# Where the output products of the last column groups stand, in a six-layer decoder kernel on one core

## The chip, the cores and the metric

The kernel runs on one NeuronCore of a Trainium2 chip. The time is device time of one execution in microseconds (us); less is better. The matmul engine is called PE (its weight loads PEld), the vector engine DVE, the activation engine ACT, GpSimd POOL; SP issues the DMA transfers.

## The reference

256 tokens of width 1024, all float32. A first block of two layers, each with a hybrid mixer, a cross attention on a memory and a squared-ReLU MLP, every part followed by a layer norm; then a second block of four layers, each with a mixer (retention, dilated attention, gMLP, retention), a SwiGLU FFN and a gated embedding, with RMS norms. Cut to the parts that the change touches:

```python
def squared_relu_mlp(x, w1, w2):            # two layers; w1 1024x4096, w2 4096x1024
    h = jnp.square(jax.nn.relu(jnp.einsum('bsd,df->bsf', x, w1)))
    return jnp.einsum('bsf,fd->bsd', h, w2)

def _swiglu(h, w_in, w_out):                # four layers; hidden width 2816
    gate, up = jnp.split(h @ w_in, 2, axis=-1)
    return (jax.nn.silu(gate) * up) @ w_out

def _retention_mixer(h, w_in, w_out):       # layers 0 and 3; four heads of value width 512
    ...
    return (jax.nn.silu(g) * y) @ w_out

def _gmlp_mixer(h, w_in, ln_g, ln_b, w_s, b_s, w_out):   # layer 2; width 2048
    ...
    return (u * s) @ w_out
```

## The kernel before, in words

The 256 tokens are two tiles of 128. Each tile is a Python generator, `thread(0)` and `thread(1)`, called t0 and t1 here. All weights come from HBM in 840 **blocks** of at most 512 KB, in the order of one list, `plan`: a `colblock` is a quarter of the rows of 512 columns, a `rowblock` is 128 rows of all 1024 columns. A block is loaded into one of five raw buffers (`load`, SP), then split into a high and a low float32r part (`split`: ACT writes `wh`, DVE writes `wl`), one block ahead of t0; 14 pairs of buffers hold the split halves, two to a block.

The loop at the end of the kernel sets the order: for each block, t0 takes a step with it, then t1 takes a step with a block some places earlier (`LAGS`: 4 in `ff1`, 3 in `ff2`, 1 in `rv`, `rg` and `gu`, 2 in `ro` and `go`, 5 in `fg` and `fu`, 4 in `fo`). A step is six products of 128x512 by `mm3` (high by high, high by low, low by high, for two halves).

An MLP, FFN, retention or gMLP goes by **column groups**. For group j the kernel computes the inputs (`in`: `proj` into a PSUM bank `pj`; four blocks in the MLP and the gMLP, eight in the FFN and the retention), makes the hidden values, and turns them by DMA, since the next product needs them transposed. This **trip** (`turn_by_dma`, `trip`) is: a DVE transpose of 32x32 pieces, four writes of 64 KB to DRAM (`xd<-xt`), one read back (`ffr<-xd`, `ffu<-xd`, `ro<-xd`, `gor<-xd`), and the split into the parts of the transposed operand (`part`, by ACT and DVE). The read back is put off until one step of the same thread later and the split until three steps later (`BACK, CUT = 1, 3`, counted by `flush`). Then the **output products** (`out`: `outproj`, accumulated in two PSUM banks `acc`; four blocks, two in the last group of the FFN, which is 256 wide) take the parts.

Before, the order within each of these stages is in 0, in 1, out 0, in 2, out 1, and so on, with the last two output groups behind the last input:

```python
for j in range(9):
    if j < 8:
        p = yield from proj(t, xT, ("ff1", l, j), 512)
        ...
        turn_by_dma(t, r_, 4, fT, j, IALPHA ** 0.5)
    if j > 0:
        yield from outproj(t, acc, ("ff2", l, j - 1), 4, fT, 4 * j - 4, j == 1, j == 8, ...)
```

After the last output product of a thread comes a norm (`layer_norm`, or `postnorm` and `prenorm`), whose result is transposed on PE (`xTp`) and split into the next stage's `part`. The transposed parts have eight buffers a thread: four pairs, of which the stage's own input `xT` holds two as long as inputs are left. The order of instructions on each engine follows this text with small shifts that the tile framework's scheduler makes; DVE, ACT, PE and the SP queue each work strictly in their order.

Of the kernel before, what the change touches and what calls it, by code (L numbers as in the profile page):

```python
# [15 lines left out]
P = 128  # L16
# [32 lines left out]
def kernel(  # L49
# [18 lines left out]
    tiles = {}  # L68
    shared = {}


    plan = []

# [7 lines left out]
    def rowblock(key, mat, kts):  # L81
        v = mat.rearrange("(k p) n -> p k n", p=P)
        for i, k in enumerate(kts):
            plan.append((key + (i,), "w", [P, 1, D], v[:, k:k + 1, :], None))
# [19 lines left out]
    for l in range(2):  # L104
        for nm, c0, n in MIXG:
            if nm == "cq" and l == 0:
                for t in range(2):
                    aux(("memr", t), "kv", [P, D], mem[t * P:(t + 1) * P, :])
            if nm == "cq":
                aux(("BT", l), "big8", [P, 6, 256], relx[l])  # L110
            colblock((nm, l), w_in[l], c0, n)
        for j in memory_blocks(l, "M"):
            colblock(("mkv", l, j), w_mkv[l], 512 * j, 512)
        rowblock(("mix", l), w_mix[l], MIXK)
        for which in range(3):
            if which == 0:
                fill(l, 0)
            if which == 1:
                for j in range(2):
                    colblock(("mq", l, j), w_mq[l], 512 * j, 512)  # L120
            if l == 1 and which == 2:
                aux(("lnGB",), "big8", [P, 2, D], bcast_row(ln_rows[l, which:which + 1, :, :]))
            if which == 1:
                rowblock(("mo", l), w_mo[l], list(range(8)))
                fill(l, 1)
            if which == 2:
                for j in range(9):
                    if j < 8:
                        colblock(("ff1", l, j), w_ff1[l], 512 * j, 512)
                    if j > 0:  # L130
                        rowblock(("ff2", l, j - 1), w_ff2[l], list(range(4 * j - 4, 4 * j)))
                fill(l, 2)
    FG = [(512 * j, min(512, 2816 - 512 * j)) for j in range(6)]
    for i in range(4):
        if i % 3 == 0:
            r = i // 3
            aux(("cb", i), "big8", [P, CB_W], cb)
            for nm, c0 in (("rq", 0), ("rk", 1024)):
                for j in range(2):
                    colblock((nm, i, j), ret_in[r], c0 + 512 * j, 512, (i, 0))  # L140
            for h in range(5):
                if h < 4:
                    colblock(("rv", i, h), ret_in[r], 2048 + 512 * h, 512, (i, 0))
                    colblock(("rg", i, h), ret_in[r], 4096 + 512 * h, 512, (i, 0))
                if h > 0:
                    rowblock(("ro", i, h - 1), ret_out[r], list(range(4 * h - 4, 4 * h)))
        elif i == 1:
            for hf in range(2):
                for g in range(3):
                    aux(("db", hf, g), "big8", [P, 8, 256], dilx[g, hf])  # L150
                    for c, nm in enumerate(("dq", "dk", "dv")):
                        colblock((nm, hf, g), att_in[0], 3072 * g + 1024 * c + 512 * hf, 512, (1, 0))
            for hf in range(2):
                rowblock(("do", hf), att_out[0], list(range(4 * hf, 4 * hf + 4)))
        else:
            aux(("gmg",), "big8", [P, 2048], bcast_row(gm_ln[0:1, :]))
            aux(("gmb",), "big8", [P, 2048], bcast_row(gm_ln[1:2, :]))
            aux(("gws",), "kv", [P, 8, P], gm_ws.rearrange("g n m -> n g m"))
            for j in range(4):
                colblock(("gv", j), gm_in[0], 2048 + 512 * j, 512, (2, 0))  # L160
            for j in range(5):
                if j < 4:
                    colblock(("gu", j), gm_in[0], 512 * j, 512, (2, 0))
                if j > 0:
                    rowblock(("go", j - 1), gm_out[0], list(range(4 * j - 4, 4 * j)))
        aux(("ng", i, 0), "grow", [P, D], bcast_row(ng_rows[i, 0:1, :]))
        for j in range(7):
            if j < 6:
                c0, n = FG[j]
                colblock(("fg", i, j), ffn_in[i], c0, n, (i, 1))  # L170
                colblock(("fu", i, j), ffn_in[i], 2816 + c0, n, (i, 1))
            if j > 0:
                c0, n = FG[j - 1]
                rowblock(("fo", i, j - 1), ffn_out[i], list(range(c0 // P, (c0 + n) // P)))
        aux(("ng", i, 1), "grow", [P, D], bcast_row(ng_rows[i, 1:2, :]))
        rowblock(("pp", i), ple_p[i], [0, 1])
        for j in range(2):
            colblock(("pg", i, j), ple_g[i], 512 * j, 512, (i, 2))
# [696 lines left out]
    def mlp(t, l, xT):  # L875
        acc = newacc(t)
        fT = Parts()
        for j in range(9):
            if j < 8:
                p = yield from proj(t, xT, ("ff1", l, j), 512)  # L880
                r_ = sb.tile([P, 512], F32, tag=f"rA{t}", name="ffr", bufs=2)
                V.tensor_scalar(out=r_, in0=p, scalar1=0.0, scalar2=None, op0=ALU.max)
                fT.banks.append(None)
                turn_by_dma(t, r_, 4, fT, j, IALPHA ** 0.5)
            if j > 0:
                yield from outproj(t, acc, ("ff2", l, j - 1), 4, fT, 4 * j - 4, j == 1, j == 8, xT if j == 1 else None)
        return acc


# [5 lines left out]
    def retention(t, i, hT, rs):  # L895
# [33 lines left out]
                turn_to(t, xf, 4, qT[j] if nm == "rq" else get2(("rkT", i, j), [P, 2, 4, P], "kv", 4)[:, t])  # L929
        acc = newacc(t)  # L930
        oT = Parts()
        for h in range(5):
            if h < 4:
                p = yield from proj(t, hT, ("rv", i, h), 512)
                vv = get2(("rv", i, h, t), [P, 512], f"U{t}", 3)
                S.activation(vv, p, AF.Copy, scale=rs[:, 0:1])
# [28 lines left out]
                V.scalar_tensor_tensor(out=o, in0=y, scalar=rr[:, 0:1], in1=th, op0=ALU.mult, op1=ALU.mult)  # L965
                oT.banks.append(None)
                turn_by_dma(t, o, 4, oT, h)
            if h > 0:
                yield from outproj(t, acc, ("ro", i, h - 1), 4, oT, 4 * h - 4, h == 1, h == 4)
        return acc  # L970

    def dilated(t, hT, rs):
# [95 lines left out]
    def gmlp(t, hT, rs):  # L1068
# [31 lines left out]
            (V if j == 0 else G).tensor_tensor(out=vs[j], in0=vs[j], in1=gb[:, sl], op=ALU.add)  # L1100
        acc = newacc(t)
        oT = Parts()
        for j in range(5):
            if j < 4:
                p = yield from proj(t, hT, ("gu", j), 512)
                u = sb.tile([P, 512], F32, tag=f"rA{t}", name="gur", bufs=2)
                S.activation(u, p, AF.Gelu, scale=rs[:, 0:1])
                sp = bank("tr", t, [P, 2, 256], "gsp")
                o = sb.tile([P, 512], F32, tag=f"rB{t}", name="gor", bufs=2)
                for k in range(2):  # L1110
                    g = 2 * j + k
                    T.matmul(sp[:, k, :], wsT[:, g, :], vs[j][:, 256 * k:256 * k + 256], start=True, stop=True)  # L1112
                for k in range(2):
                    g = 2 * j + k
                    V.scalar_tensor_tensor(out=o[:, 256 * k:256 * k + 256], in0=sp[:, k, :], scalar=gbs[:, g:g + 1],
                                           in1=u[:, 256 * k:256 * k + 256], op0=ALU.add, op1=ALU.mult)
                oT.banks.append(None)
                turn_by_dma(t, o, 4, oT, j)
            if j > 0:
                yield from outproj(t, acc, ("go", j - 1), 4, oT, 4 * j - 4, j == 1, j == 4)  # L1120
        return acc

    def swiglu(t, i, hT, rs):
# [4 lines left out]
        fT = Parts()  # L1128
        pT = shared[("pT", i, t)] = Parts()
        pT.banks.append(None)  # L1130
        for j in range(7):
            if j == 3:

                pr = sb.tile([P, 256], F32, tag=f"sc{t}", name="pr")
                nc.sync.dma_start(pr, p2[i, t * P:(t + 1) * P, :])
            if j == 4:
                turn_by_dma(t, pr, 2, pT, 0, at=21)
            if j < 6:
                n = FG[j][1]
                nkk = n // P  # L1140
                pg = yield from proj(t, hT, ("fg", i, j), n)
                th = sb.tile([P, 512], F32, tag=f"rA{t}", name="fth", bufs=2)[:, :n]
                S.activation(th, pg[:, :n], AF.Tanh, scale=hr[:, 0:1])
                V.scalar_tensor_tensor(out=th, in0=th, scalar=1.0, in1=pg[:, :n], op0=ALU.add, op1=ALU.mult)
                pu = yield from proj(t, hT, ("fu", i, j), n, PU)
                f = sb.tile([P, 512], F32, tag=f"rB{t}", name="ffu", bufs=2)[:, :n]
                V.scalar_tensor_tensor(out=f, in0=pu[:, :n], scalar=sc[:, 0:1], in1=th, op0=ALU.mult, op1=ALU.mult)
                fT.banks.append(None)
                turn_by_dma(t, f, nkk, fT, j)
            if j > 0:  # L1150
                yield from outproj(t, acc, ("fo", i, j - 1), FG[j - 1][1] // P, fT, 4 * j - 4, j == 1, j == 6)
        return acc

    def embedding(t, i):
# [180 lines left out]
```

## Time and profile before

| what | value |
|---|---|
| time, median of 3 runs | 2572.3 us (2567.38 to 2573.31) |
| the profiled execution's own time | 2566.06 us |
| span of that execution (first to last instruction) | 2564.3 us |
| PE busy | 2521.9 us, 98% of the span, 12100 matmuls |
| PEld busy | 2059.6 us, 80% |
| DVE busy | 1823.3 us, 71% |
| ACT busy | 1501.9 us, 59% |
| DMA, mean of the span | 206 GB/s |

Matmuls overlap on PE, and a matmul's end in the profile is modelled: busy time is an upper measure of how full PE is. "Idle before" is the time between the end of one instruction and the start of the next on the same engine, with the instruction that ended the wait.

### The profile page before, as it was taken

The numbers are of one execution on the slowest core, as the hardware profiler recorded it, in microseconds if no ns is written. First come the engines' busy times: TensorE is split into PE (matmuls) and PEld (weight loads), VectorE is DVE, ScalarE is ACT, GpSimd is POOL, SyncE is SP. The second block draws the span as 40 slices with busy tenths as digits, with TensorE's granted clock in tenths as the row PEclk, the third lists the DMA queues.
The fourth block names the chain that finished last, engine by engine and source line by source line (L and its number), as shares of the span: only waits on it lengthen the run. The fifth ranks groups of instructions, "written<-read, shape, count | busy, mean of one in ns | idle before, by whom it ended". The sixth has DMA issues, their size and how long they took to land. (4 is left out here: it accounts for less than half of the span.)

```text
span 2564.3 us, 36170 instructions
## 1 busy us (share of the span) xinstructions
PE 2521.9 (98%) x12100; PEld 2059.6 (80%) x12100; DVE 1823.3 (71%) x3357; ACT 1501.9 (59%) x2856; POOL 60.0 (2%) x88
## 2 busy tenths in 40 slices
PE   8999999999999999999999999999999999999999
PEld 7787787887788778788777787888877887887887
DVE  8865767866766876766866767767767678766666
ACT  6653555654455565555766666557656557565555
POOL 0000000000000000000000000000100000000000
PEclk9999999999999999999999999999999999999999
DMA  6463776554578677677766665777576776766774
GB/s 214 150 215 103 224 245 187 171 192 156 155 233 244 190 235 248 190 240 219 221 204 209 194 208 179 230 214 223 170 257 212 226 221 196 255 220 193 230 208 159
DMA packets 321227, 528.27 MB, mean 206 GB/s; under 512 B 37392, under 2 KB 135824, under 8 KB 319888
## 3 DMA queue, kind: packets, MB, share of 16 engines
q1 hardware_dynamic: 321040, 525.96, 66.4%
q8 instruction: 95, 1.56, 0.3%
q14 instruction: 92, 0.75, 0.1%
HBM read 484.96 MB, written 40.89 MB: 205 GB/s over the span
## 5 line engine op out<-in xcount | busy, mean ns | idle before, releaser
L326 PE MATMUL pj<-wh,part 128*128 128x512 f32 (+3 forms) x4480 | 1415.4, 384 | 4.9 <-ACT part L284 1.4
L326 PEld LDWEIGHTS pj<-wh,part 128*128 128x128 f32 x4480 | 831.2, 188 | 174.3 <-issue 8.9
L326 PE MATMUL pj<-wl,part 128*128 128x512 f32 (+3 forms) x2240 | 852.9, 381 | 1.3 <-DVE wl L228 1.3
L326 PE MATMUL acc<-wh,part 128*128 128x512 f32 x1920 | 582.2, 395 | 12.8 <-ACT part L284 5.9
L326 PEld LDWEIGHTS pj<-wl,part 128*128 128x128 f32 x2240 | 421.9, 188 | 79.1 <-DVE wl L228 2.7
L326 PEld LDWEIGHTS acc<-wh,part 128*128 128x128 f32 x1920 | 356.8, 189 | 92.5 <-ACT part L284 8.4
L326 PE MATMUL acc<-wl,part 128*128 128x512 f32 x960 | 307.1, 393 | 0.1
L232 DVE TENSOR_TENSOR wl<-ff,wh 128x512 fp32r<-128x512 f32 x256 | 169.6, 686 | 102.9 <-ACT wh L284 102.6
L284 ACT CAST wh<-ff 128x512 fp32r<-128x512 f32 x256 | 152.4, 620 | 131.5 <-PE acc L326 64.6
L326 PEld LDWEIGHTS acc<-wl,part 128*128 128x128 f32 x960 | 180.8, 188 | 38.3 <-DVE wl L232 0.6
L225 ACT ACTIVATE wh<-fg,ngc 128x512 fp32r<-128x512 f32 (+1 forms) x192 | 126.5, 686 | 116.3 <-PE pj L326 60.7
L228 DVE SCALAR_TENSOR_TENSOR wl<-fg,ngc,wh 128x512 fp32r<-128x512 f32 (+1 forms) x192 | 129.5, 702 | 74.2 <-ACT wh L225 74.1
L228 DVE SCALAR_TENSOR_TENSOR wl<-fu,ngc,wh 128x512 fp32r<-128x512 f32 (+1 forms) x192 | 128.1, 704 | 53.8 <-ACT wh L225 47.9
L225 ACT ACTIVATE wh<-fu,ngc 128x512 fp32r<-128x512 f32 (+1 forms) x192 | 123.5, 684 | 62.2 <-PE acc L326 38.5
L284 ACT CAST wh<-fo 128x512 fp32r<-128x512 f32 x176 | 103.7, 621 | 76.9 <-PE pj L326 72.4
L232 DVE TENSOR_TENSOR wl<-fo,wh 128x512 fp32r<-128x512 f32 x176 | 114.9, 685 | 42.2 <-ACT wh L284 39.5
L232 DVE TENSOR_TENSOR wl<-mkv,wh 128x512 fp32r<-128x512 f32 x64 | 41.9, 687 | 27.0 <-ACT wh L284 26.9
L228 DVE SCALAR_TENSOR_TENSOR wl<-rg,ngc,wh 128x512 fp32r<-128x512 f32 x64 | 44.9, 748 | 19.7 <-ACT wh L225 19.6
L284 ACT CAST wh<-mkv 128x512 fp32r<-128x512 f32 x64 | 37.5, 620 | 36.2 <-PE acc L326 21.2
L228 DVE SCALAR_TENSOR_TENSOR wl<-pg,ngc,wh 128x512 fp32r<-128x512 f32 x64 | 46.3, 748 | 15.9 <-ACT wh L225 15.4
L225 ACT ACTIVATE wh<-rv,ngc 128x512 fp32r<-128x512 f32 x64 | 43.2, 718 | 21.6 <-PE pj L326 9.3
L232 DVE TENSOR_TENSOR wl<-ro,wh 128x512 fp32r<-128x512 f32 x64 | 42.8, 686 | 18.1 <-ACT wh L284 18.0
(315 smaller groups left out, 3175.8 us busy)
## 6 DMA issues: line engine op xcount, KB each, us to landing
ff<-in_w_ff_dram SPq DMA_DIRECT2D x128, 512.0 KB, 4.4
fo<-in_ffn_out_dram SPq DMA_DIRECT2D x88, 512.0 KB, 4.4
fg<-in_ffn_in_dram SPq DMA_DIRECT2D x80, 512.0 KB, 4.5
fu<-in_ffn_in_dram SPq DMA_DIRECT2D x80, 512.0 KB, 4.3
xd<-xt SPq DMA_DIRECT2D x576, 64.0 KB, 2.4
mkv<-in_w_mkv_dram SPq DMA_DIRECT2D x32, 512.0 KB, 4.6
rv<-in_ret_in_dram SPq DMA_DIRECT2D x32, 512.0 KB, 5.5
rg<-in_ret_in_dram SPq DMA_DIRECT2D x32, 512.0 KB, 4.2
```

What stands on the lines that cost most here:

```text
L225: S.activation(h_, r_, AF.Copy, scale=gc)
L228: V.scalar_tensor_tensor(out=l_, in0=r_, scalar=gc, in1=h_.bitcast(F32), op0=ALU.mult, op1=ALU.subtract)
L232: (V if le == "v" else G).tensor_tensor(out=l_, in0=r_, in1=h_.bitcast(F32), op=ALU.subtract)
L284: S.copy(o, i)
L326: T.matmul(outs[i], a, ws[i][b], start=s0, stop=s1)
```

## The change

A function `order_of(n)` gives the order of inputs and outputs for n column groups, for the list of blocks and for the four stages alike. Out j still stands behind in j+1, but only for the groups up to n-4; the output products of the last three groups stand together behind the last group's inputs. For the MLP (n = 8) the end becomes in 5, out 4, in 6, in 7, out 5, out 6, out 7, where it was in 5, out 4, in 6, out 5, in 7, out 6, out 7. For the FFN (n = 6): in 3, out 2, in 4, in 5, out 3, out 4, out 5. For retention and gMLP (n = 4): in 0, in 1, out 0, in 2, in 3, out 1, out 2, out 3. No instruction is added or removed. In the FFN the split of the small tile `pr`, for the embedding, is due after 18 steps and not after 21.

```diff
+    def order_of(n):
+        seq = [("in", 0)]
+        for j in range(1, n):
+            seq.append(("in", j))
+            if j < n - 2:
+                seq.append(("out", j - 1))
+        return seq + [("out", j) for j in range(max(n - 3, 0), n)]
...
             if which == 2:
-                for j in range(9):
-                    if j < 8:
+                for what, j in order_of(8):
+                    if what == "in":
                         colblock(("ff1", l, j), w_ff1[l], 512 * j, 512)
-                    if j > 0:
-                        rowblock(("ff2", l, j - 1), w_ff2[l], list(range(4 * j - 4, 4 * j)))
+                    else:
+                        rowblock(("ff2", l, j), w_ff2[l], list(range(4 * j, 4 * j + 4)))
...
     def mlp(t, l, xT):
         acc = newacc(t)
         fT = Parts()
-        for j in range(9):
-            if j < 8:
+        for what, j in order_of(8):
+            if what == "in":
                 p = yield from proj(t, xT, ("ff1", l, j), 512)
...
-            if j > 0:
-                yield from outproj(t, acc, ("ff2", l, j - 1), 4, fT, 4 * j - 4, j == 1, j == 8, xT if j == 1 else None)
+            else:
+                yield from outproj(t, acc, ("ff2", l, j), 4, fT, 4 * j, j == 0, j == 7, xT if j == 0 else None)
...
     def swiglu(t, i, hT, rs):
-        for j in range(7):
-            if j == 3:
+        for what, j in order_of(6):
+            if (what, j) == ("in", 3):
...
-            if j == 4:
-                turn_by_dma(t, pr, 2, pT, 0, at=21)
-            if j < 6:
+            if (what, j) == ("in", 4):
+                turn_by_dma(t, pr, 2, pT, 0, at=18)
+            if what == "in":
...
-            if j > 0:
-                yield from outproj(t, acc, ("fo", i, j - 1), FG[j - 1][1] // P, fT, 4 * j - 4, j == 1, j == 6)
+            else:
+                yield from outproj(t, acc, ("fo", i, j), FG[j][1] // P, fT, 4 * j, j == 0, j == 5)
```

The plan's lists for the FFN, the retention and the gMLP, and the loops of `retention` and `gmlp`, are changed in the same way.

The first place is the end of the MLP of layer 0, on ACT, which splits the blocks (`wh<-ff`, the digits behind are layer, group and block) and the turned groups (`ffT`, `part`). Before, the split of t1's last group (`part_4472`) stands behind three blocks of the next stage (`mkv`):

```order
L284 CAST wh<-ff_0_7_1_4285 128x512 x2
L284 CAST wh<-ff_0_7_2_4317 128x512
L394 ACTIVATE ffT<-ffr 128x512
L284 CAST wh<-ff_0_7_2_4317 128x512
L284 CAST part_4384<-ffT 128x512
L284 CAST wh<-ff_0_7_3_4346 128x512 x2
L284 CAST wh<-mkv_0_0_4368 128x512 x2
L284 CAST wh<-mkv_0_1_4405 128x512 x2
L284 CAST wh<-mkv_0_2_4428 128x512 x2
L394 ACTIVATE ffT<-ffr 128x512
L284 CAST part_4472<-ffT 128x512
```

After the change, the same piece of ACT's order. Here `part_4296` is t0's last group, `part_4274` t1's group 6 and `part_4384` t1's last group:

```order
L403 ACTIVATE ffT<-ffr 128x512
L293 CAST wh<-ff_0_6_2_4222 128x512
L293 CAST part_4296<-ffT 128x512
L403 ACTIVATE ffT<-ffr 128x512
L293 CAST wh<-ff_0_6_3_4252 128x512
L293 CAST part_4274<-ffT 128x512
L293 CAST wh<-ff_0_6_3_4252 128x512
L293 CAST wh<-ff_0_7_0_4280 128x512 x2
L293 CAST wh<-ff_0_7_1_4317 128x512 x2
L293 CAST wh<-ff_0_7_2_4340 128x512 x2
L403 ACTIVATE ffT<-ffr 128x512
L293 CAST part_4384<-ffT 128x512
```

The split of t0's last group has moved from block 2 of out 7 to block 2 of out 6, four blocks earlier, and that of t1's last group from block 2 of the next stage to block 2 of out 7; t0's last and t1's last but one now follow each other at once.

The second place is the end of the MLP of layer 1, on DVE, where t0's layer norm begins (`bn`, `mv`, `ve`, `x`) beside the splits of retention's first blocks (`wl<-rq`, the digits are layer of the second block, group and block). Before:

```order
L228 SCALAR_TENSOR_TENSOR wl<-rq_0_2_8835,ngc,wh 128x512
L538 BN_STATS bn_8923<-acc_7150 128x6
L538 BN_STATS bn_8923<-acc_7151 128x6
L228 SCALAR_TENSOR_TENSOR wl<-rq_0_2_8835,ngc,wh 128x512
L315 TENSOR_TENSOR part_8880<-ffT,part_8879 128x512
L540 BN_AGGR mv_8926<-bn_8923 128x2
L542 TENSOR_SCALAR ve_8928<-mv_8926 128x1
L550 TENSOR_SCALAR x_8932<-acc_7150,mv_8926,rs_8930 128x512
```

After the change, the same piece:

```order
L237 SCALAR_TENSOR_TENSOR wl<-rq_0_2_8841,ngc,wh 128x512
L547 BN_STATS bn_8923<-acc_7150 128x6
L547 BN_STATS bn_8923<-acc_7151 128x6
L237 SCALAR_TENSOR_TENSOR wl<-rq_0_2_8841,ngc,wh 128x512
L549 BN_AGGR mv_8926<-bn_8923 128x2
L237 SCALAR_TENSOR_TENSOR wl<-rq_0_3_8863,ngc,wh 128x512
L551 TENSOR_SCALAR ve_8928<-mv_8926 128x1
L237 SCALAR_TENSOR_TENSOR wl<-rq_0_3_8863,ngc,wh 128x512
L559 TENSOR_SCALAR x_8932<-acc_7150,mv_8926,rs_8930 128x512
```

The split of t1's last group (`part_8880`) no longer stands in the norm; the two halves of the weight block `rq_0_3` have moved up into it.

## Rows read from the trace of the kernel before

**Rows 1.** Page, parts 5 and 6: output products; the trip's writes, us to landing

```profile
L326 PE MATMUL acc<-wh,part 128*128 128x512 f32 x1920 | 582.2, 395 | 12.8 <-ACT part L284 5.9
...
xd<-xt SPq DMA_DIRECT2D x576, 64.0 KB, 2.4
```

**Rows 2.** Busy time by stretch: span, engines (x instructions), clock, DMA share, GB/s

```profile
269.00:281.00 12.00, 12.00 (x63) 10.20 (x62) 8.94 (x14) 6.22 (x12) 0.00 (x0) 1.00 0.83 256
303.00:412.00 109.00, 109.00 (x482) 90.26 (x482) 71.09 (x110) 59.08 (x100) 0.00 (x0) 1.00 0.78 240
...
848.00:852.00 4.00, 3.64 (x10) 2.94 (x11) 2.87 (x6) 1.41 (x3) 0.55 (x1) 0.59 0.49 135
...
1210.00:1218.00 8.00, 8.00 (x58) 7.42 (x58) 6.12 (x13) 5.37 (x12) 0.00 (x0) 1.00 0.94 317
```

**Rows 3.** PE's waits of the whole span: us in total, times, longest

```profile
PE acc L326 <- ACT part L284: 5.9, 6, 2.8
PE acc L326 <- ACT part L397: 4.9, 4, 1.4
```

**Rows 4.** PE's waits at the end of MLP 0, 412 to 440 us

```profile
PE acc L326 <- ACT part L284: 1.9, 2, 1.0
PE xTp L572 <- DVE z L568: 0.3, 1, 0.3
```

**Rows 5.** PE's waits at the end of MLP 1, 835 to 872 us

```profile
PE acc L326 <- ACT part L284: 3.0, 2, 2.8
PE pj L326 <- DVE part L315: 1.1, 1, 1.1
PE pj L326 <- ACT part L284: 0.7, 1, 0.7
PE xTp L279 <- DVE x L553: 0.6, 1, 0.6
```

**Rows 6.** PE's timeline: start, us, [idle before]; FFN 0, both retentions' ends

```profile
1039.66 0.72 PE L326 MATMUL acc<-wh,part 128*128 128x512 f32 x2 [1.42 <-ACT part L397]
...
1228.37 0.72 PE L326 MATMUL acc<-wh,part 128*128 128x512 f32 x2 [0.80 <-ACT part L397]
...
2331.38 0.73 PE L326 MATMUL acc<-wh,part 128*128 128x512 f32 x2 [1.30 <-ACT part L397]
```

**Rows 7.** PE's timeline at the first output group of MLP 0 and of the gMLP

```profile
282.05 0.73 PE L326 MATMUL acc<-wh,part 128*128 128x512 f32 x2 [0.50 <-ACT part L284]
...
1863.57 0.73 PE L326 MATMUL acc<-wh,part 128*128 128x512 f32 x2 [1.37 <-ACT part L397]
```

**Rows 8.** Timeline: the trip of t1's last group in MLP 0

```profile
413.55 0.69 DVE L882 TENSOR_SCALAR ffr<-pj 128x512 f32<-128x512 f32 x1
...
418.04 1.80 SPq L364 DMA_DIRECT2D xd<-xt  x4
...
427.18 0.63 ACT L394 ACTIVATE ffT<-ffr 128x512 f32<-128x512 f32 x1 [1.10 <-DMA ffr<-xd]
...
428.51 0.73 PE L326 MATMUL acc<-wh,part 128*128 128x512 f32 x2 [0.89 <-ACT part L284]
```

**Rows 9.** Timeline: end of MLP 1, t0's layer norm and t1's last products

```profile
845.45 1.29 DVE L538 BATCH_NORM_STATS2 bn<-acc 128x6 f32<-128x512 f32 x2
...
848.34 0.69 DVE L315 TENSOR_TENSOR part<-ffT,part 128x512 fp32r<-128x512 f32 x1 [0.95 <-ACT part L284]
848.36 1.22 PE L326 MATMUL acc<-wh,part 128*128 128x512 f32 x2 [2.79 <-ACT part L284]
...
850.10 1.53 DVE L550 TENSOR_SCALAR x<-acc,mv,rs 128x512 f32<-128x512 f32 x2 [0.76 <-POOL rs L289]
...
852.74 1.29 DVE L553 TENSOR_TENSOR x<-x,lnGB 128x512 f32<-128x512 f32 x2
...
854.63 0.60 PE L279 MATMUL xTp<-tab,x 128*128 128x128 f32 x4
...
856.38 0.50 PE L326 MATMUL pj<-wh,part 128*128 128x512 f32 x1
```

More of the change, by code (lines that the diff above doesn't have):

```diff
@@ L140 @@
                     colblock((nm, i, j), ret_in[r], c0 + 512 * j, 512, (i, 0))
-            for h in range(5):
-                if h < 4:
+            for what, h in order_of(4):
+                if what == "in":
                     colblock(("rv", i, h), ret_in[r], 2048 + 512 * h, 512, (i, 0))
                     colblock(("rg", i, h), ret_in[r], 4096 + 512 * h, 512, (i, 0))
-                if h > 0:
-                    rowblock(("ro", i, h - 1), ret_out[r], list(range(4 * h - 4, 4 * h)))
+                else:
+                    rowblock(("ro", i, h), ret_out[r], list(range(4 * h, 4 * h + 4)))
         elif i == 1:
@@ L160 @@
                 colblock(("gv", j), gm_in[0], 2048 + 512 * j, 512, (2, 0))
-            for j in range(5):
-                if j < 4:
+            for what, j in order_of(4):
+                if what == "in":
                     colblock(("gu", j), gm_in[0], 512 * j, 512, (2, 0))
-                if j > 0:
-                    rowblock(("go", j - 1), gm_out[0], list(range(4 * j - 4, 4 * j)))
+                else:
+                    rowblock(("go", j), gm_out[0], list(range(4 * j, 4 * j + 4)))
         aux(("ng", i, 0), "grow", [P, D], bcast_row(ng_rows[i, 0:1, :]))
-        for j in range(7):
-            if j < 6:
-                c0, n = FG[j]
+        for what, j in order_of(6):
+            c0, n = FG[j]
+            if what == "in":
                 colblock(("fg", i, j), ffn_in[i], c0, n, (i, 1))
                 colblock(("fu", i, j), ffn_in[i], 2816 + c0, n, (i, 1))
-            if j > 0:
-                c0, n = FG[j - 1]
-                rowblock(("fo", i, j - 1), ffn_out[i], list(range(c0 // P, (c0 + n) // P)))
+            else:
+                rowblock(("fo", i, j), ffn_out[i], list(range(c0 // P, (c0 + n) // P)))
         aux(("ng", i, 1), "grow", [P, D], bcast_row(ng_rows[i, 1:2, :]))
@@ L877, in mlp @@
         fT = Parts()
-        for j in range(9):
-            if j < 8:
+        for what, j in order_of(8):
+            if what == "in":
                 p = yield from proj(t, xT, ("ff1", l, j), 512)
@@ L884, in mlp @@
                 turn_by_dma(t, r_, 4, fT, j, IALPHA ** 0.5)
-            if j > 0:
-                yield from outproj(t, acc, ("ff2", l, j - 1), 4, fT, 4 * j - 4, j == 1, j == 8, xT if j == 1 else None)
+            else:
+                yield from outproj(t, acc, ("ff2", l, j), 4, fT, 4 * j, j == 0, j == 7, xT if j == 0 else None)
         return acc
@@ L931, in retention @@
         oT = Parts()
-        for h in range(5):
-            if h < 4:
+        for what, h in order_of(4):
+            if what == "in":
                 p = yield from proj(t, hT, ("rv", i, h), 512)
@@ L967, in retention @@
                 turn_by_dma(t, o, 4, oT, h)
-            if h > 0:
-                yield from outproj(t, acc, ("ro", i, h - 1), 4, oT, 4 * h - 4, h == 1, h == 4)
+            else:
+                yield from outproj(t, acc, ("ro", i, h), 4, oT, 4 * h, h == 0, h == 3)
         return acc
@@ L1102, in gmlp @@
         oT = Parts()
-        for j in range(5):
-            if j < 4:
+        for what, j in order_of(4):
+            if what == "in":
                 p = yield from proj(t, hT, ("gu", j), 512)
@@ L1118, in gmlp @@
                 turn_by_dma(t, o, 4, oT, j)
-            if j > 0:
-                yield from outproj(t, acc, ("go", j - 1), 4, oT, 4 * j - 4, j == 1, j == 4)
+            else:
+                yield from outproj(t, acc, ("go", j), 4, oT, 4 * j, j == 0, j == 3)
         return acc
@@ L1130, in swiglu @@
         pT.banks.append(None)
-        for j in range(7):
-            if j == 3:
+        for what, j in order_of(6):
+            if (what, j) == ("in", 3):
                 pr = sb.tile([P, 256], F32, tag=f"sc{t}", name="pr")
                 nc.sync.dma_start(pr, p2[i, t * P:(t + 1) * P, :])
-            if j == 4:
-                turn_by_dma(t, pr, 2, pT, 0, at=21)
-            if j < 6:
+            if (what, j) == ("in", 4):
+                turn_by_dma(t, pr, 2, pT, 0, at=18)
+            if what == "in":
                 n = FG[j][1]
@@ L1149, in swiglu @@
                 turn_by_dma(t, f, nkk, fT, j)
-            if j > 0:
-                yield from outproj(t, acc, ("fo", i, j - 1), FG[j - 1][1] // P, fT, 4 * j - 4, j == 1, j == 6)
+            else:
+                yield from outproj(t, acc, ("fo", i, j), FG[j][1] // P, fT, 4 * j, j == 0, j == 5)
         return acc
```

## The prediction

> **What bounds the kernel now.** I read the page first: PE is busy for 98% of the span, so the kernel is bound by the number of matmuls, and only PE's waits can be won. The busy time by stretch says how evenly they lie. In the middle of MLP 0, 303 to 412 us, PE has no idle time: 482 matmuls in 109 us, one per 0.226 us, at the full clock, with DVE at 65% and the DMA engines at 78% [rows 2]. There the order of inputs and outputs can win nothing. So the question is the ends.
>
> The waits of PE over the whole span come next. Output products (`acc`) wait for the split of a turned group (`part`) for 5.9 us in six places and 4.9 us in four [rows 3]. I looked where the ten lie. Seven, 8.4 us in all, are at ends: two at the end of MLP 0 (1.9 us) [rows 4], two at that of MLP 1 (3.0 us) [rows 5], one at the end of each retention (1.42 and 1.30 us) and one at that of FFN 0 (0.80 us) [rows 6]. The other three are at the first output group, out 0, of the MLPs and the gMLP (0.50 us, the like in MLP 1, and 1.37 us) [rows 7]; these stand behind in 1 before and after, and stay. The ends of FFN 1 to 3 and of the gMLP show no such wait.
>
> The timeline of one trip shows why. DVE takes t1's last group of MLP 0 out of PSUM at 413.55; the writes are issued from 418.04; the read back has landed at 427.18; the first product starts at 428.51 after a wait of 0.89 [rows 8]. A trip takes 15.0 us. Between the last input and the last output group stands one group of outputs: four blocks of two threads, 48 matmuls, 10.8 us, and a little more. The waits are what is missing.
>
> **The change, part by part.** It removes no work and adds none.
>
> *The cover of a trip.* After the change two output groups of both threads stand between the last input and its output: 96 matmuls, 21.7 us, against 15.0: 6.7 us to spare. For the last group but one an input and an output group stand there, which is as much. In the FFN out 3 and out 4 cover in 5: eight blocks of t0 at 1.36 us and eight of t1, which are at worst all of width 256, at 0.83 us (six matmuls of 0.138 us, from 58 in 8.00 us [rows 2]), 17.5 us. So all seven waits go: 8.4 us. A wait counts from the modelled end of the matmul before, 0.395 us after its start [rows 1], where the next could have started after 0.226; each costs 0.17 us more than shown. By place: MLP 0 1.9 + 0.3 = 2.2; retentions 2.72 + 0.34 = 3.1; FFN 0 0.80 + 0.17 = 1.0 us. MLP 1 is a case of its own.
>
> *MLP 1.* t1's wait there is 2.79 us [rows 9], and after it the granted clock is 0.59 in the stretch 848 to 852, between the two levels of 1.2 and 2.4 GHz: ten matmuls take 3.64 us, not 2.3 [rows 2]. The clock fell after 2.79 us without matmuls and none of the shorter waits (1.42 us at most) did that. But behind t1's products PE has nothing until t0's layer norm is done, and it is not early: from t0's last product (845.4, when the norm's statistics start) to the first product of the next stage (856.38) are 11.0 us [rows 9]. After the change t1's 24 products end 5.4 us after t0's, and PE waits for the norm. Before, from the start of the statistics to the whole of x are 8.6 us (845.45 to 854.03). Out of DVE's way goes t1's split (`part` at 848.34: 0.95 us of waiting and 0.69); into it come two halves of `rq_0_3`, some 0.7 each like the other operations of this size there, one of them inside the 0.76 us that DVE waited for POOL [rows 9]: 8.6 - 1.6 + 1.0, about 8.0 us. The first half of x is there some 0.6 sooner, at 7.4, and from the first transpose to the next stage's first product are 1.75 us (854.63 to 856.38) [rows 9]: 9.1, and a product that needs the low part, behind those halves on DVE, some 0.2 later. So that stage starts 11.0 - 9.3 = 1.7 us earlier. t0's own out 7 also loses its small wait, 0.2 us and the 0.17, some 0.3 us. Behind this come t1's own norm and three waits of 1.1, 0.7 and 0.6 us [rows 5]; its statistics then come 5.4 us earlier against t0's stream, but the same DVE has t0's work first: I take half, 1.2 us; bounds 0 and 2.4. MLP 1: 3.2 us, with 0.3 to 5.4 as bounds (below: t0's gain is eaten by a clock that falls in the new wait).
>
> *MLP 0.* Its norm is hidden better, since t0's `mkv` products don't need it. The wait for `z`, 0.3 us [rows 4], grows by 0.2: a half of `mkv_0_3` moves up in front of it on DVE. 2.0 us remain.
>
> *Retentions.* The removed wait lies ahead of t0's last products and all of what follows moves with it; no cover is lost. 3.1 us.
>
> *Two inputs in succession.* This is what is new in the middle: in 6 and in 7, in 4 and in 5, in 2 and in 3. t0's last trip and t1's last but one then fall together, as the order of ACT shows. The same meeting is there before, at in 0 and in 1: in MLP 0 from 269 to 281 PE is busy 12.00 of 12.00 us at 256 GB/s [rows 2]. So I cost it at nothing in the MLPs, the retention and the gMLP. In the FFN it meets blocks half as wide, consumed in half the time: 1210 to 1218 has DMA engines 94% busy at 317 GB/s [rows 2], with PE still full. Two more trips of 512 KB (four writes of 64 KB and a read of 256 KB) come into this stretch: 3.3 us of transfers at that rate in each of the four FFNs. The five raw buffers cover that (at 1.36 us and more a block, 6.8 us); I take 0.2 us an FFN, 0.8 in all, and 0 to 13.2 as bounds. The earlier split of `pr` lies on ACT and DVE between weight splits and costs nothing.
>
> Sum: 2.0 + 3.2 + 3.1 + 1.0 - 0.8 = 8.5 us. From the profiled execution's 2566.06 us this gives 2557.6. The median of the runs is 6.2 us above that execution, so I predict 2572.3 - 8.5, about 2564 us.
>
> A rule speaks against all this. The row first: from the issue of the writes to the landing of the read are 9.1 us [rows 8], though one write by itself lands 2.4 us after its issue [rows 1]. The Trainium skill, DMA: Bandwidth & Descriptors, section Anatomy of one DMA, gives a transfer a fixed cost of about 2 us plus its bytes over the peak rate. By that a trip's two dependent transfers would be, as an estimate, some 5 us, parts would be there before their products even now, and the change would win nothing (a rival, below). The trace disagrees by 4 us: the read is issued behind loads on SP, and its bytes run among theirs.
>
> **The rivals.**
>
> *The wait moves on to the norms.* Where the parts come in time, the next chain ends last. For it: MLP 1, where PE waits for x already [rows 5]; a wait of some 2 us, two transposes and another wait follow, so the clock may fall again (1.4 us), and t1's waits may stay. Against it: MLP 0 and the retentions have other products to run. Then MLP 1 gives 0.3, the FFN nothing, and the retentions half: 2.0 + 0.3 + 1.5 = 4 us less, about 2568.
>
> *The two inputs in succession starve PE in the FFNs (slower).* One mechanism: the half-wide blocks at 94% DMA. If the raw buffers don't cover the 3.3 us, that is four times 3.3, 13.2, less 9.3 won: 4 us slower. To be slower by over 0.3% (7.7 us) each stall must reach 4.3 us; with a falling clock as in rows 2, 1.4 us each, it is 18.8 - 9.3, 9.5 us slower, 2582. Against it: PE stood full at 317 GB/s. The Trainium skill, TensorE: Matmul & The Clock Gate, section What's actually happening, has it that the clock is lowered unless activity holds it up, which agrees with the fall after 2.79 us; it makes such stalls dearer than they look.
>
> *The change doesn't do what it says.* By a trip of 2.4 us for the write and the like for the read, 5 us, the parts' lateness comes from the place of read and split in the queues, counted in steps of the thread, and moves along with the outputs: the waits stay, 2572. Against it: in the middle of the MLPs, where 21.7 us stand between, none is seen [rows 2].
>
> **How the numbers follow.** 0.3% of the time, 7.7 us, is about what a measurement of this kernel can tell from no change. My forecast has 0.62: 0.50 for over 7.7 us and 0.12 for a little under, since 8.5 is close to it. The wait that moves on: 0.22, within 0.3%. The starved FFN: 0.11, of which 0.07 beyond 0.3% and 0.04 within. No effect: 0.05. So faster 0.50, same 0.43, slower 0.07. The range: below, the lowest run, 2567.4, less 12 us (all terms at their upper bound: 2.2 + 5.4 + 3.1 + 1.0); above, 2574, a little over the highest run shown, which takes in the rivals at 2568 and 2572 and leaves out the starved FFN. The forecast alone: 2558 to 2567.
>
> **What would show it.** Right: no wait of `acc` for a `part` at the seven places; trips still of 13 to 16 us; three waits at out 0 as before; clock 1.00 around the end of MLP 1, and there a wait of some 2 us of `xTp` for `x`; PE full in the stretches of two inputs. Wrong: a `wl` or `wh` that PE waits for at the FFNs' half-wide blocks, loads that land late there, a clock of 0.5 anywhere new, or the waits for `part` still there.

## The result, and the profile after

The changed kernel takes 2549.76 us (median of 4 runs, 2548.18 to 2553.86); the kernel before took 2569.84 us in the four runs beside it (2566.45 to 2573.31). The ratio is 0.9926, with a 95% interval of 0.9911 to 0.9941: 20 us faster, 0.74%. I had forecast faster as the likeliest sign, but 2564 us, with a range that began at 2555: the gain by the runs' medians is more than twice my sum of 8.5 us, that between the two profiled executions twice. The profiled execution took 2549.19 us, with a span of 2547.5: 16.9 us less than that of before (2566.06).

The page of the changed kernel: PE's busy time, the output products [rows 1] and the trip's writes.

```profile
PE 2516.1 (99%) x12100; PEld 2061.2 (81%) x12100; DVE 1820.0 (71%) x3357; ACT 1501.5 (59%) x2856; POOL 59.5 (2%) x88
...
L335 PE MATMUL acc<-wh,part 128*128 128x512 f32 x1920 | 568.7, 393 | 4.3 <-DVE part L327 1.9
...
xd<-xt SPq DMA_DIRECT2D x576, 64.0 KB, 2.4
```

PE's waits over the whole span of the changed kernel: in total, times, longest (lines are 9 higher than before).

```profile
PE xTp L288 <- DVE x L562: 2.1, 2, 1.8
...
PE acc L335 <- DVE part L327: 1.9, 4, 0.7
...
PE acc L335 <- ACT part L406: 1.4, 1, 1.4
...
PE acc L335 <- ACT part L293: 1.1, 2, 0.9
...
PE pj L335 <- ACT embh L1170: 0.2, 1, 0.2
```

Of the ten waits of [rows 3] the three at out 0 are left (1.4 and 1.1 us); the seven at the ends are gone, as forecast. The idle time in front of the output products fell from 12.8 to 4.3 us, 8.5 us, where I had counted 8.4. But the time fell by twice that. The spans say where the rest hides: PE stood still for 2564.3 - 2521.9 = 42.4 us before and 2547.5 - 2516.1 = 31.4 after, 11.0 us less, and its busy time fell by 5.8 us, although the 12,100 matmuls are the same. A matmul's modelled end lies 0.17 us behind the earliest start of the next (0.395 against 0.226), so a pause up to that length shows as busy time, and a longer one 0.17 us too short.

So I read starts instead. The n-th matmul is taken in both traces, at two points around each end where both have done the same work, and the starts are subtracted. For FFN 1, for instance, the first product of t0's embedding (`pep`) moved from 1754.44 to 1745.61, that of t1's from 1771.06 to 1761.09: 8.83 and then 9.97 us, so 1.1 us were won between the two. Before:

```profile
1754.44 0.61 PE L326 MATMUL pep<-wh,part 128*128 128x512 f32 x2
...
1771.06 0.40 PE L326 MATMUL pep<-wh,part 128*128 128x512 f32 x1
```

The table gives what each end won (the forecast without its 0.8 us for two inputs in succession) against the profiled execution of before, in us (a minus is faster), in the changed kernel, in a second trace of it (`e9_control`) and in the experiments below.

| end of | forecast | after | e9 | e1 | e2 | e3 | e4 | e5 |
|---|---|---|---|---|---|---|---|---|
| MLP 0 | -2.0 | -3.0 | -3.0 | -0.7 | -3.0 | -3.0 | -3.1 | -3.0 |
| MLP 1 | -3.2 | -2.9 | -2.9 | -1.7 | -2.1 | -2.9 | -2.9 | -2.2 |
| retention 0 | -1.55 | -1.7 | -1.7 | -0.5 | -1.6 | -1.4 | -1.7 | -1.7 |
| FFN 0 | -1.0 | -2.3 | -2.2 | -2.2 | 0.6 | -2.2 | -1.2 | -2.2 |
| FFN 1 | 0 | -1.5 | -1.5 | -1.6 | 0.6 | -1.5 | -0.6 | -1.5 |
| gMLP | 0 | -2.1 | -2.2 | -2.1 | 0.0 | -2.1 | -2.1 | -2.1 |
| FFN 2 | 0 | -1.2 | -1.1 | -0.5 | 0.0 | -0.2 | 0.4 | -1.2 |
| retention 3 | -1.55 | -1.8 | -1.7 | 0.5 | -1.7 | -1.8 | -1.7 | -1.7 |
| FFN 3 | 0 | -1.7 | -1.7 | -1.7 | -0.5 | -1.7 | -0.7 | -1.7 |

The nine ends give 18.2 us; the stages between them lost 1.4 us from one of these two executions to the other. FFN 1 to 3 and the gMLP, which I had costed at nothing, give 6.5 of them.

What is there to see at such an end? FFN 1, PE's timeline of before, around t0's embedding:

```profile
1756.25 0.39 PE L326 MATMUL acc<-wl,part 128*128 128x512 f32 x1
1756.76 0.66 PE L279 MATMUL xTp<-tab,x 128*128 128x128 f32 x4
...
1760.90 0.39 PE L326 MATMUL pep<-wh,part 128*128 128x512 f32 x1
1761.52 0.50 PE L326 MATMUL pj<-wh,part 128*128 128x512 f32 x1 [0.23 <-ACT embh L1161]
```

From 1756.25 to 1756.76 are 0.51 us where 0.226 would do, and no wait is shown; from 1760.90 to 1761.52 are 0.62, and 0.23 is shown. The same place in the changed kernel:

```profile
1753.11 0.39 PE L335 MATMUL pep<-wh,part 128*128 128x512 f32 x1
1753.34 0.39 PE L335 MATMUL acc<-wh,part 128*128 128x512 f32 x1
...
1754.47 0.39 PE L335 MATMUL acc<-wh,part 128*128 128x512 f32 x1
1754.70 0.39 PE L335 MATMUL pj<-wh,part 128*128 128x512 f32 x1
```

Six products of t1's last group (`acc`) now stand between t0's `pep` and its gate product `pj`; meanwhile ACT copies `pep` out of its PSUM bank (`embh`), which the gate product needs free, and the gate product starts without a pause. Before, t1's products stood behind the gate's first ones. That this place follows from the late part is what e4 below tests.

The other FFN ends are alike. By PE's starts, each of the four has three pauses before: 0.28 us beyond the pitch of 0.226 ahead of the transposes of t0's `x` for the gate, 0.36 to 0.39 ahead of the first gate product, and 0.29 to 0.30 ahead of the transposes of t1's `x`; 0.93 us and a little more in all. Ahead of these FFN 0 has 0.96 us and FFN 1 0.28 us for a `part`, and FFN 3 0.32 us for the low half of a weight block. In the changed kernel none of these pauses is left.

At the gMLP's end it is t1's norm. Before:

```profile
1943.05 0.39 PE L326 MATMUL acc<-wh,part 128*128 128x512 f32 x1
...
1946.51 0.63 PE L279 MATMUL xTp<-tab,x 128*128 128x128 f32 x4 [0.62 <-DVE x L606]
1947.81 0.50 PE L326 MATMUL pj<-wh,part 128*128 128x512 f32 x1 [0.68 <-ACT part L284]
```

After:

```profile
1926.47 0.39 PE L335 MATMUL acc<-wh,part 128*128 128x512 f32 x1
...
1933.09 0.60 PE L288 MATMUL xTp<-tab,x 128*128 128x128 f32 x4
1933.44 0.48 PE L335 MATMUL pj<-wh,part 128*128 128x512 f32 x1
```

From t1's last output product to the transposes of its next input were 3.5 us, and PE waited for `x` and then for the `part`; now there are 6.6 us full of t0's products, and both waits are gone.

### The profile page after: what moved, and what is told of

Same layout as the page of the kernel before. It is cut to its first block, busy times and chain, and to the rows that moved or that the text cites. A ratio compares the mean times of both kernels' runs of the same rounds, so it can differ in the third digit from the quotient of the medians.

```text
span 2547.5 us, 36189 instructions
## 1 busy us (share of the span) xinstructions
PE 2516.1 (99%) x12100; PEld 2061.2 (81%) x12100; DVE 1820.0 (71%) x3357; ACT 1501.5 (59%) x2856; POOL 59.5 (2%) x88
## 5 line engine op out<-in xcount | busy, mean ns | idle before, releaser
L335 PE MATMUL acc<-wh,part 128*128 128x512 f32 x1920 | 568.7, 393 | 4.3 <-DVE part L327 1.9
L234 ACT ACTIVATE wh<-rg,ngc 128x512 fp32r<-128x512 f32 x64 | 42.9, 717 | 18.9 <-PE pj L335 8.0
L241 DVE TENSOR_TENSOR wl<-ro,wh 128x512 fp32r<-128x512 f32 x64 | 42.4, 685 | 15.3 <-ACT wh L293 15.3
```

What stands on the lines that cost most here:

```text
L234: S.activation(h_, r_, AF.Copy, scale=gc)
L241: (V if le == "v" else G).tensor_tensor(out=l_, in0=r_, in1=h_.bitcast(F32), op=ALU.subtract)
L335: T.matmul(outs[i], a, ws[i][b], start=s0, stop=s1)
```

## The experiments

Three theories stood against each other. **T**, mine: only the waits for late parts at the seven places, perhaps mis-sized. **N**: the late parts also held t1's last products back on PE, and with them the next stage. **P**: the earlier split of `pr` did it at the FFNs.

**e1_ffn_gmlp and e2_mlp_ret: one half of the change each.** `order_of` gets the number of groups held back; 2 is the old order. e1:

```diff
-    def order_of(n):
+    def order_of(n, hold=3):
...
-        for what, j in order_of(8):
+        for what, j in order_of(8, 2):
...
-        for what, h in order_of(4):
+        for what, h in order_of(4, 2):
```

e2 has `order_of(6, 2)` in the FFNs (with `at=21`) and `order_of(4, 2)` in the gMLP instead.

> The new order in the four FFNs and the gMLP alone; the MLPs and the retentions keep the old one. Three theories. Theory T (trips): the whole gain is that PE no longer waits for a late part at the seven places that I counted, and the sizes there were too small. By it this kernel gains only FFN 0's 1.0 us less what two inputs in succession cost, 0 to 1 us in all (ratio to before 1.000). Theory N (next stage): the late parts of the last groups also kept t1's last output products behind the next stage's products on PE, so that t1's norm and the embedding began late, and this shows as short waits of other tiles, many hidden in matmuls that look busy. By it all four FFN ends and the gMLP's end gain, 2.25, 1.55, 1.2, 1.7 and 2.1 us by the starts of the stages in the two traces: 8.8 us (0.9966). Theory P (pr): the FFN ends gain by the earlier split of pr: some 6.7 us here, and the gMLP nothing.

> The new order in the two MLPs and the two retentions alone; the FFNs and the gMLP keep the old one, and pr its split after 21 steps. Theory T: all that the change brings, 16 to 20 us, since these places hold 7.4 of the 8.4 us of counted waits. Theories N and P: what is left when the 8.8 us of the FFNs and the gMLP are taken away, 9 to 10 us by the starts of the stages (3.0 at each MLP, 1.8 and 1.85 at the retentions): ratio 0.996.

e1 took 2558.96 us (2555.42 to 2563.05) and e2 2558.55 (2557.1 to 2559.5), beside 2567.77 for before (10 runs): ratios 0.9965 (0.9953 to 0.9977) and 0.9964 (0.9951 to 0.9976). That is 8.8 and 9.2 us, together 18.0. T falls: it gave e1 at most 1 us, and e1's interval begins at 5.9. In the table the FFN and gMLP ends gain in e1 what they gain in the whole change (FFN 2 less), and in e2 move by 0.6 us either way.

e1 shows something else at MLP 1, where it has the old order. PE's timeline at its wait for t1's part:

```profile
848.00 0.73 PE L333 MATMUL acc<-wh,part 128*128 128x512 f32 x2 [2.06 <-ACT part L291]
```

The stretch behind it (span, engines, granted clock, DMA share, GB/s):

```profile
848.00:852.00 4.00, 4.00 (x18) 3.31 (x19) 3.21 (x7) 2.51 (x4) 0.55 (x1) 1.00 0.47 134
```

The wait was 2.06 us and not 2.79 [rows 9], and the clock stayed at 1.00; this end lost 1.7 us less than in the profile that I predicted from, with the same order.

**e3_pr_late: the split of `pr` due after 21 steps again.**

```diff
-                turn_by_dma(t, pr, 2, pT, 0, at=18)
+                turn_by_dma(t, pr, 2, pT, 0, at=21)
```

> The changed kernel with the split of pr due after 21 steps again, not 18. Theory P: the unforeseen gain at the FFN ends goes, 1.1 us at each, some 4.6 us of the whole (ratio to before some 0.995). Theories T and N: nothing moves by more than 0.5 us against the changed kernel (0.9926 to 0.9935).

2550.31 us, ratio 0.9929 (0.9916 to 0.9943), and the ends of FFN 0, 1 and 3 keep their 2.2, 1.5 and 1.7 us. P falls. FFN 2, which varies by a microsecond among these traces, has lost its three pauses here too. What it loses in e3 lies earlier, at the two inputs in succession, where PE waits for the low half of a half-wide weight block:

```profile
2072.18 0.83 PE L335 MATMUL pj<-wh,part 128*128 128x512 f32 x2
2073.34 0.39 PE L335 MATMUL pj<-wl,part 128*128 128x256 f32 x1 [0.33 <-DVE wl L237]
```

From start to start that is 0.8 us lost in e3; at the same place it is 0.5 us in e1 (whose split is due after 18 steps) and 0.3 in e4, and nothing in the changed kernel.

**e4_t1_trip_late and e5_t0_trip_late: one thread's last trip late again.** For the last group of the FFN, and in the same way of the gMLP (e5: `t == 0`):

```diff
-                turn_by_dma(t, f, nkk, fT, j)
+                if t == 1 and j == 5:
+                    put_off(t, 4, lambda f=f: turn_by_dma(1, f, 2, fT, 5))
+                else:
+                    turn_by_dma(t, f, nkk, fT, j)
```

> The changed kernel, but the whole trip of t1's last group, in the FFNs and the gMLP alone, starts four steps of t1 later, so that again one group of output products covers it, as before; t0's trips and the order of blocks are the changed kernel's. Theory N: the part is late again, t1's last output products stand again among the first gate products of the embedding, and the FFN ends give back 0.8 to 1.2 us each, 3 to 5 us in all; the gMLP's end gives back little, since on PE its t1 products keep their new place. Theory T: only FFN 0 had a counted wait, so at most 1 us comes back. If t0's trips were what mattered, nothing comes back.

> The companion of the run with t1's trip late: the changed kernel, but in the FFNs and the gMLP the whole trip of t0's last group starts four steps of t0 later, t1's trips as in the changed kernel. If the FFN ends gain through t1's last products alone (what gave back about 1.0 us an FFN in that run), nothing comes back here. If t0's last products count as well (the rest of the gain, 1.2 us in FFN 0 and some 0.2 to 0.7 in the others), that rest comes back, 2 to 3 us in all. The gMLP's end gives back nothing by either, since the order on PE stays there.

e4 took 2552.38 us, 0.9942 (0.9929 to 0.9954); e5 2550.57, 0.9932 (0.9915 to 0.9948). In e4 each FFN end gives back about a microsecond (1.1, 0.9 and 1.0 at FFN 0, 1 and 3; at FFN 2 0.6 against e3, 1.6 against the change), the gMLP nothing; in e5 none of the ends that it edits gives back anything. So of the two trips it is t1's that counts at the FFNs, not t0's. By the runs alone this would not be clear: e4's median lies 2.1 us above that of e3, measured beside it, with intervals that overlap; the traces carry it. Around t0's gate in FFN 1, e4 has t1's products among the gate's again, and a pause of 0.52 us from start to start, of which nothing is shown as a wait. It stands in front of the first product of t1's late part, which ACT finishes at 1753.01:

```profile
1752.54 0.39 PE L335 MATMUL pep<-wh,part 128*128 128x512 f32 x1
1753.06 0.73 PE L335 MATMUL acc<-wh,part 128*128 128x512 f32 x2
...
1754.10 0.39 PE L335 MATMUL pj<-wh,part 128*128 128x512 f32 x1
1754.32 0.86 PE L335 MATMUL acc<-wh,part 128*128 128x512 f32 x3
```

In each FFN e4 has back 0.21 us of pause ahead of t0's transposes, 0.30 for the late part itself and 0.27 to 0.30 ahead of t1's transposes, some 0.8 us. What the ends keep in e4 (1.2, 0.6 and 0.7 us at FFN 0, 1 and 3) came back with neither trip alone. By PE's starts it is above all the pause ahead of the gate product, 0.36 to 0.39 us, since in e4 four products of t1 still stand there, and the pauses for a `part` in FFN 0 and FFN 1. Which piece of the change holds these stays open.

**e6_before_t1_early: the kernel before, t1's last block of the gMLP earlier.**

```diff
-        while done <= n - LAGS.get(order[n][0], LAG):
+        lag = 2 if order[n] in (("fg", 2, 0, 0), ("fg", 2, 0, 1)) else LAGS.get(order[n][0], LAG)
+        while done <= n - lag:
```

> The kernel before, with nothing of the change, but at the end of the gMLP t1's last output block stands 18 products of t0 earlier on PE, behind block 1 of the FFN's first input and not behind block 4. Theory N: the gMLP's end gained because this block stands earlier, so that t1's norm begins earlier; then some 1.8 us of the 2.1 us come here too, without the change. Theory T, or a gain that comes from the order of the blocks or their loads: nothing at this place, or a wait for the part of up to 2 us. The rest of the kernel stays as before: ratio 0.999 to 1.000.

2568.67 us against 2568.17, ratio 0.9998 (0.9987 to 1.001), and 0.3 us at the place itself, not 1.8. PE's timeline there says why:

```profile
1941.46 0.39 PE L326 MATMUL acc<-wh,part 128*128 128x512 f32 x1
...
1944.92 1.29 PE L279 MATMUL xTp<-tab,x 128*128 128x128 f32 x8 [0.36 <-DVE x L606]
1946.48 0.50 PE L326 MATMUL pj<-wh,part 128*128 128x512 f32 x1 [0.27 <-ACT part L284]
```

t1's transposes moved forward along with its last block: 3.5 us lie between the two, as before. My expectation named the wrong quantity. It isn't where the block stands that counts but how much of t0's work lies between it and the transposes that need its norm: 10 products before, 12 here, 28 in the changed kernel. The two waits sum to 1.30, 0.63 and 0 us. That is consistent, but I had no kernel that sets this distance alone, so for the gMLP it is argued, not shown. By the letter of the expectation, nothing at this place is what a gain from the order of the blocks would give; this run doesn't exclude it.

**e7_ff2_lag5 and e8_two_behind: two attempts to win more.** e7 changes `"ff2": 3` in `LAGS` to 5. e8 runs the MLPs and the gMLP by

```python
    def two_behind(n):
        seq = [("in", 0), ("in", 1)]
        for j in range(2, n):
            seq += [("in", j), ("out", j - 2)]
        return seq + [("out", n - 2), ("out", n - 1)]
```

> The changed kernel with t1 five blocks behind t0 in the MLP's output products, not three. At the end of MLP 1 twelve more products of t1 (2.7 us) are left for the time in which PE waits 1.8 us for t0's x. If that wait is all that is left of the norm's chain there, 1.5 to 2 us are won (ratio to before some 0.992 where the changed kernel had 0.9926); if t1's own norm is then late for its first products, it comes back there and nothing is won.

> The changed kernel with the output products two groups behind the inputs all through the MLPs and the gMLP (in 0, in 1, in 2, out 0, in 3, out 1, and so on), the split of a group due after five steps where it would otherwise find no free buffer. By the waits of the changed kernel's trace, those for the part at the first output group (1.1 us in two places and 1.4 us in one, with some 0.5 us hidden) go: 2 to 3 us less than the changed kernel, ratio to before some 0.9915. Against: two inputs in succession at the start, and parts that stay longer in their buffers, could make the split wait: then up to as much more.

e7: 2548.1 us, 0.9923 (0.9907 to 0.9939); e8: 2549.04, 0.9925 (0.991 to 0.994). Neither can be told from the change, and what was expected of them didn't come. In e7 the end of MLP 1 gains 4.0 us and not 2.9, and that of MLP 0 2.5 and not 3.0: t0's wait for `x` at MLP 1 fell from 1.80 to 0.27 us, but t1's rose to 1.59:

```profile
845.98 1.26 PE L288 MATMUL xTp<-tab,x 128*128 128x128 f32 x8 [0.27 <-DVE x L562]
...
858.78 0.63 PE L288 MATMUL xTp<-tab,x 128*128 128x128 f32 x4 [1.59 <-DVE x L562]
```

In e8 the waits for the part at out 0 are gone, and PE's waits of its whole span have others that were not there:

```profile
PE pj L341 <- ACT wh L299: 1.3, 2, 0.6
...
PE pj L341 <- ACT gur L1122: 0.9, 1, 0.9
```

**e9_control, e10_lag5_gmlp, e11_lag5_gmlp_rq5.** The changed kernel once more; with e7's edit and e8's for the gMLP alone; and that with `"rq": 4` changed to 5.

> The changed kernel itself once more, unaltered, beside the two that build on it: ratio to before 0.991 to 0.994.

> The changed kernel with the two edits whose profiles showed something at their place: t1 five blocks behind in the MLP's output products (1.1 us at the end of MLP 1) and the gMLP's outputs two groups behind its inputs (0.7 us at its first output group). If they add up, 1.8 us less than the control, ratio to before some 0.9920 where the control has 0.9926; the difference to the control can be at the edge of what the runs tell.

> The run before with t1 five blocks behind in the retention's first inputs as well, not four. With five blocks in the MLP's outputs t1's x came 1.59 us late there. This leaves two more products of t0 (0.45 us) ahead of t1's transposes, so 0.4 us more is won, or nothing if the split of the weights waits for a free buffer.

2548.52 us, 0.9925 (0.9912 to 0.9937); 2548.48, 0.9921 (0.9909 to 0.9934); 2549.77, 0.993 (0.9916 to 0.9943). No version is better than the change by more than the runs tell; the 1.8 us expected of e10 aren't there. In e10's trace the clock also fell in the dilated attention, 0.53 in the stretch 1532 to 1536, which none of its edits touches and where the changed kernel had 1.00. e11 lost at MLP 1: t1's wait there grew to 3.50 us in PE's timeline.

```profile
861.18 0.63 PE L294 MATMUL xTp<-tab,x 128*128 128x128 f32 x4 [3.50 <-DVE x L568]
```

The clock fell behind it, by the busy time in two stretches of e11:

```profile
860.00:864.00 4.00, 2.14 (x11) 1.77 (x12) 3.20 (x7) 2.28 (x6) 0.55 (x1) 0.88 0.55 100
864.00:868.00 4.00, 4.00 (x14) 3.17 (x13) 2.87 (x7) 2.86 (x5) 0.00 (x0) 0.70 0.73 293
```

## Why the prediction was wrong

**The step that failed** is "the ends of FFN 1 to 3 and of the gMLP show no such wait", from which I costed them at 0, and with it FFN 0 at its one shown wait, 1.0 us. They measured 1.5, 1.2, 1.7 and 2.1 us, and FFN 0 2.3: 7.8 us that the sum didn't have. I looked for one pair, `acc` for `part`, in a list of waits. A late part has a second price: the products that need it stand further back in PE's order, what hangs on them (t1's norm, the gate behind the embedding) loses its cover, and PE pauses for other tiles. e1 shows the size; e4 and e5 show that at the FFNs about 1 us each hangs on t1's last trip, of which 0.3 us is the late part itself, in a pause too short for the list, and 0.5 us the pauses for `x`. Of the 8.8 us of these five ends the waits of before show some 2.9: 0.80 for the part in FFN 0, 0.2 for `embh` in each FFN, 1.30 at the gMLP. The rest were pauses too short for the list, and the hidden part of the longer ones: counted from start to start, pauses of over 0.12 us beyond the pitch sum to 7.9 us at these five ends before and 1.0 us after.

**What held.** The seven waits went and the three at out 0 stayed. *MLP 1* gave 2.9 for my 3.2, with the forecast exchange: PE no longer waits for the part but 1.80 us for t0's `x`, and the clock stays at 1.00. In the changed kernel's profile:

```profile
844.00:848.00 4.00, 4.00 (x19) 3.13 (x17) 3.56 (x7) 3.95 (x7) 0.90 (x1) 1.00 0.59 153
848.00:852.00 4.00, 2.13 (x12) 1.44 (x12) 4.00 (x8) 3.24 (x8) 0.00 (x0) 1.00 0.37 125
```

That the clock held was luck in part. e2 and e5 have the changed order at this place and the same wait, 1.79 us, and behind it their clock fell, to 0.61 and 0.57 in the stretch 852 to 856; there the end won 2.1 and 2.2 us. In e3, e4 and e9 it held, as in the changed kernel's first profile. In e2:

```profile
849.89 1.26 PE L286 MATMUL xTp<-tab,x 128*128 128x128 f32 x8 [1.79 <-DVE x L560]
...
852.00:856.00 4.00, 4.00 (x13) 3.10 (x12) 3.95 (x12) 0.26 (x1) 0.55 (x1) 0.61 0.48 131
```

The *retentions* gave 3.5 for 3.1. *MLP 0* gave 3.0 for 2.0: mis-sized, and part of that is the one profile, since the old order loses 0.7 to 1.8 us less there in e1 and e6. *Two inputs in succession* cost 0 and not 0.8 in the changed kernel's profile: in FFN 0 PE is full through in 4 and in 5 and through the outputs behind, where the DMA engines are 95% busy. But the sign of being wrong that I had named, a `wl` that PE waits for at the half-wide blocks, did show at FFN 2 in e1, e3 and e4, with 0.3 to 0.8 us.

```profile
1170.00:1205.00 35.00, 35.00 (x198) 30.68 (x197) 24.97 (x45) 21.41 (x41) 0.00 (x0) 1.00 0.69 204
1205.00:1223.00 18.00, 18.00 (x84) 14.99 (x83) 11.65 (x22) 10.02 (x21) 0.00 (x0) 1.00 0.95 307
```

**The trip** itself got little shorter. t1's last group of MLP 0 leaves PSUM at 403.83, its writes are issued from 406.37, and its part is done at 417.02 + 0.69: 13.9 us, now under 21.7 us of products. Before, the part was done at 428.49 + 0.69, 15.6 us (the 15.0 of the prediction go to the first product). The difference lies ahead of the writes, which were issued 2.5 us after the group left PSUM and not 4.5; from there to the finished part it is 11.3 us after and 11.1 before.

```profile
403.83 0.69 DVE L891 TENSOR_SCALAR ffr<-pj 128x512 f32<-128x512 f32 x1
...
406.37 2.54 SPq L373 DMA_DIRECT2D xd<-xt  x4
...
417.02 0.69 DVE L324 TENSOR_TENSOR part<-ffT,part 128x512 fp32r<-128x512 f32 x1 [1.16 <-ACT part L293]
```

**The rivals.** That the wait moves on to the norms happened at MLP 1 alone. There it cost what I had already taken off, and where the clock fell, in e2 and e5, 0.7 to 0.8 us more; the rival had 1.4. Starved FFNs are ruled out by the windows of FFN 0 above and by the FFN ends, which all won, and "the change doesn't do what it says" by the waits that went. Beside the last stood a page: the Trainium skill, DMA: Bandwidth & Descriptors, Anatomy of one DMA, gives a fixed cost of about 2 us a transfer. That section is on the path by GpSimd, which the prediction didn't say, while these transfers are issued by SP. By that cost the trips were never late; the trace disagrees here as before, since the seven waits ended when the trips were covered.

**The bounds.** The range began at the lowest run less 12 us, the upper bounds of the terms that I had; a term that is missing has no bound in it. (The 5.4 that it has for MLP 1 is itself more than its shown terms, 1.7, 0.3 and 2.4, which sum to 4.4.) The sum was taken from 2572.3 us, the median of three runs; with the fourth it was 2569.84, and in the later sets 2567.8 to 2568.4, so some 2 to 4 us of the miss lie in the start. And one trace of before was taken as the kernel, where that execution was 3.8 us under the median of its four runs: the runs of before spread over 11.4 us (2563.61 to 2574.99, 17 runs on one chip) and, in two other sets, over 9.1 and 6.6. The changed kernel's nine, in two sets, spread over 6.1 (2547.75 to 2553.86), but e5's six over 7.8 and e10's five over 8.1, so that the new order repeats better as a whole isn't shown. At the retentions the traces differ: with the old order a retention's end took up to 2.6 us more (e6) in one execution than in another; with the new one the two repeat within 0.3 us. A term that rests on a wait for a trip wants a bound of some 1 to 2 us at each place, by an estimate from these differences.

## What to carry to other kernels

When a late operand is taken out of an in-order engine's way, price not only the waits that name it but the place of its products in the order, and what follows them: count how much other work lies between the last product of one stage and the first instruction that needs its norm. Where an engine is 98% busy with overlapped instructions, measure from start to start, not by idle time; here 5.8 of 16.8 us had been counted as busy. And take a term that rests on a DMA's lateness from several executions, or give it their spread.

## What the runs showed of the hardware

Behind PE's waits the granted clock fell in some cases and not in others. In e6, MLP 1's wait for the part was 2.70 us, until 846.98; the busy time by stretch there:

```profile
844.00:848.00 4.00, 1.30 (x5) 0.83 (x4) 3.06 (x7) 1.31 (x3) 0.00 (x0) 0.86 0.52 164
848.00:852.00 4.00, 4.00 (x14) 3.22 (x13) 3.29 (x6) 2.00 (x4) 0.55 (x1) 0.71 0.30 114
```

0.71 there, 0.70 behind the 3.50 us of e11, 0.69 behind 2.33 us at e6's last retention, 0.59 behind the 2.79 us of before [rows 2], all between the levels of 1.2 and 2.4 GHz; behind 2.24 us at e6's first retention, 2.06 in e1 and 1.80 in the changed kernel it stayed at 1.00. But the length of the wait doesn't decide it alone: behind the 1.79 us of e2 and e5 it fell as well (the rows of e2 stand above).

So a wait can cost more than its length, and the same wait in the same order does so in one execution and not in another: MLP 1's end differs by 0.7 to 0.8 us between the changed kernel and these two, and by 1.7 us between two traces of the old order whose waits differ by 0.73. The Trainium skill, TensorE: Matmul & The Clock Gate, What's actually happening, says that the throttled state is the default and that activity releases it; the falls behind PE's waits agree.
